# A hybrid RWKV-7 / S5 layer on one core: GpSimd's key products, PSUM tiles of one bank, the merge's loads and the rank of the chain

## The chip, the core and the metric

The kernel runs on one NeuronCore of a Trainium2 chip. The core has five engines that work at the same time, each through its own queue in order: TensorE (PE in the profile; its weight loads are listed as PEld), VectorE (DVE), ScalarE (ACT), GpSimd (POOL) and SyncE (SP), which here only starts DMA transfers. GpSimd starts some transfers too. Operands lie in SBUF, matmul results in PSUM, which has eight banks of 512 float32 columns on 128 partitions. GpSimd doesn't read PSUM in this kernel.

The metric is the device time of one execution in microseconds (us). Lower is better.

## What is computed

One decoder layer in float32 for 1024 positions of width 1024. The part that the change touches is the RWKV-7 branch: 8 heads of 64, with a state matrix per head that is decayed and corrected at every position, merged with an S5 branch under two gates.

```python
h = rms_norm(x, norm_mix_pre)
proj = h @ w_in                     # r, k, v, low-rank downs | S5 input | two gates
...
a = sigmoid(a0 + ad @ a2)
kk = k * k_k; kk = kk / norm(kk)    # per head
k = k * (1.0 + (a - 1.0) * k_a)
y = wkv7_scan(r, decay, k, v, -kk, kk * a)
y = groupnorm(y) * lnx_w + lnx_b
bonus = sum(r * k * r_k, axis=-1) * v
o_rwkv = ((y + bonus) * g) @ w_branch_rwkv
...
mixed = (g_rwkv * o_rwkv + g_s5 * o_s5) @ w_out
x = x + rms_norm(mixed, norm_mix_post)
f = conv_ffn(rms_norm(x, norm_ffn_pre), w_up, conv_w, conv_b, w_down)
x = x + rms_norm(f, norm_ffn_post)
```

## The kernel before

**Number format.** Large products are done as three matmuls: each float32 operand is split into a high part and a remainder (`split`, lines 226 and 227: a cast on ScalarE, a subtraction on VectorE), and high x high, high x low and low x high are added up (`mm3_steps`, lines 172 to 174). Weights are loaded as `wf` by SP, cast on ScalarE (line 156) and subtracted on VectorE (line 157). One step of `mm3_steps`, three matmuls of 128x128 by 512 columns, is called a projection step below.

**Stages.** Norm, S5 batches and the first projections; then the RWKV stage (`front_half`, second part), in which the remaining projections run as filling between the small matmuls of the RWKV branch; then the output projection, the norms and the feed-forward part.

**The RWKV stage.** It makes four passes `d`, i = 0 to 3: two groups of four heads (`g`), two halves of the sequence (`th`). For a pass,

- two *fronts* (`rwkv_front`, one for each pair of heads, u = 0 and 1) load k, tz (decay) and ta (the in-context rate) and later r and v, build the scaled keys and queries `bk` and `ar` (each [128, 8 chunks, 128], two halves of 64 columns), multiply them on TensorE into the masked matrices `gr` (line 702, evicted on line 705), and make the bonus term: a product of r, r_k and the new key, summed over each head by a matmul with a block matrix of ones (line 715). In the kernel before, the new key is made in `ta` by GpSimd (lines 690 and 691) and the product is VectorE's (line 713);
- `rwkv_inv` inverts the 32x32 diagonal blocks on VectorE (lines 760 and 762), taking them out and back through DRAM with GpSimd's DMAs (lines 710, 753, 765, 772). It is issued after the second front's end;
- `rwkv_nat` transposes keys and values, and `rwkv_level` puts the 64x64 inverse together: transposes on VectorE (line 784), two rounds of small matmuls (lines 791 and 799) with ScalarE copies between them (793 and 801);
- `rwkv_chain` goes through the eight chunks of 64 positions in order. A chunk has three bursts of small matmuls: line 832 (state S times `ar`), line 841 and the next chunk's lines 814 to 818 (`chain_v`), lines 849 and 851. Between the bursts ScalarE copies p1 (834), VectorE copies U (843) and updates S (853), ScalarE scales S (837) and copies the result yn (856). Each burst needs the eviction before it;
- `rwkv_out` normalises, adds the bonus, multiplies by g and stores the branch's result to `YR` in DRAM.

**What sets the order.** TensorE's queue has exactly the order in which the program issues its matmuls (`manual_schedule`). `drive` issues it: three lanes (the chain lane with nat, level, chain and out; two prep lanes with the fronts) and a list of fillings `self.fill` (projection steps). A lane yields a cost and a due time, and, where there is a third value, a factor. The planner has a clock `now` and a credit. A lane's step is issued if its due time is reached and the credit isn't negative; it takes 0.8 (`PACE`) x cost x factor from the credit. Otherwise one projection step is issued, which adds 0.68 to the clock and to the credit, up to 2.0 (`CREDIT`). A chain burst yields 0.6, 1.0, 0.6 with a due time of 0.8 (`T_CH`) after it. The inverse has a due time of 36.

The other engines' queues are put in order by a scheduler: among the instructions that are ready by its model, the one with the highest priority goes first. A priority is the place in the program, raised by `high_priority`: the prep lanes by `HP` (100000), the chain lane by `HP2` (200000), the fillings and `load_w` by `HPW` (400000). The inverse is issued under `HPW` too.

**The fillings of this stage.** What is left of the r, k, v projections, then 14 gate tiles one by one and two together (`gate_tiles(14, 15)`, 32 projection steps), and, put in by the chain lane after pass 1, `merge` (gates times branch results, with the S5 branch's GLU, 80 steps) and `outproj` (64 steps); after pass 3's `rwkv_nat`, `merge_s5`. `merge` begins by loading four tiles of `YR` (line 1083, by SP) into buffers with the tag `ld`, of which there are ten, and splitting them.

**PSUM in this stage.** Two banks for projections (`gm`), two for `rp`, and the chain's `cz`: two tiles of two banks. A chunk's tile z is read as [2, 4, 2, 64]: index k = 0 (p1, S and U sums, first bank), k = 1 (results, second bank).

Of the kernel before, what the change touches and what calls it, by code (L numbers as in the profile page):

```python
# [71 lines left out]
class Kern:  # L72
# [40 lines left out]
    def cz(self):  # L113

        return self.psx.tile([128, 1024], F32, tag="cz", name=self.nm("cz"), bufs=2)
# [506 lines left out]
    def rwkv_setup(self):  # L622
        nc = self.nc
        self.S = [self.rk.tile([128, 2, 64], F32, name=f"S{g}") for g in range(2)]
        for g in range(2):
            nc.gpsimd.memset(self.S[g], 0.0)

# [14 lines left out]
    def rwkv_front(self, d, u):  # L642
# [18 lines left out]
        k, tz, ta = (ld(x) for x in (self.RKV[4 + p], self.TZ[p], self.TA[p]))  # L661
# [28 lines left out]
        G.tensor_scalar(ta, ta, self.ka_h[:, p:p + 1], self.ka_1[:, p:p + 1], ALU.mult, ALU.add)  # L690
        G.tensor_tensor(ta, ta, k, ALU.mult)
        G.tensor_tensor(bk1, c64(ta), c64(tz), ALU.mult)
# [20 lines left out]
        V.scalar_tensor_tensor(r, r, self.vec("r_k", p), ta, ALU.mult, ALU.mult)  # L713
        pb = self.rp()
        mm(pb, self.cst("ones_bd"), r, start=True, stop=True)
# [58 lines left out]
    def rwkv_level(self, d):  # L774
# [3 lines left out]
        gr = d["gr"]  # L778
        p = self.cz().rearrange("p (u k c t) -> p u k c t", u=2, k=2, t=32)
# [8 lines left out]
        for u in range(2):  # L788
            for c in range(8):
                for h in range(2):  # L790
                    mm(p[hi[h], u, 0, c], gr[lo[h], u, c, h, 32:64], xz[lo[h], u, c], start=c == 0, **kw)
            for h in range(2):
                A.copy(xz[hi[h], u], p[hi[h], u, 0])
            yield 0.6, 0.3, 2.5
        yield 0, T_LV
        for u in range(2):
            for c in range(8):
                for h in range(2):
                    mm(p[lo[h], u, 1, c], xz[hi[h], u, c], gr[hi[h], u, c, h, 32:64], start=c == 0, **kw)
            for h in range(2):  # L800
                A.copy(gr[lo[h], u, :, h, 32:64], p[lo[h], u, 1])
# [3 lines left out]
    def chain_v(self, d, c):  # L805
# [3 lines left out]
        z = d["z", c] = self.cz().rearrange("p (k n u i) -> p k n u i", k=2, n=4, i=64)  # L809
        kw = dict(stop=True, skip_group_check=True)  # L810
        for u in range(2):
            for h, own in enumerate(HALF):
                sl = HALF[1 - h]
                mm(z[own, 0, 0, u], gr[sl, u, c, h, 0:64], V[sl, c, u], start=u == 0, **kw)
                mm(z[sl, 1, 0, u], gr[sl, u, c, h, 64:128], V[sl, c, u], start=u == 0, **kw)
            for h, own in enumerate(HALF):
                sl = HALF[1 - h]
                mm(z[own, 0, 1, u], bkn[sl, u, c, h], V[sl, c, u], start=False, **kw)

    def rwkv_chain(self, d):  # L820
# [6 lines left out]
        for c in range(8):  # L827
            z = d.pop(("z", c))
            for u in range(2):
                for k in range(2):  # L830
                    for h, sl in enumerate(HALF):
                        mm(z[HALF[h ^ k], k, 0, u], ar[sl, u, c, 64 * k:64 * k + 64], S[sl, u], **kw)
            p1 = self.small.tile([128, 2, 64], F32, tag="p1", name=self.nm("p1"), bufs=1)
            A.copy(p1, z[:, 0, 0])
# [3 lines left out]
            yield 0.6, T_CH  # L838
            for u in range(2):
                for h, sl in enumerate(HALF):  # L840
                    mm(z[sl, 0, 2, u], gr[sl, u, c, h, 0:64], p1[sl, u], **kw)
            U = self.small.tile([128, 2, 64], F32, tag="U", name=self.nm("U"), bufs=1)
            V.tensor_copy(U, z[:, 0, 2])
# [1022 lines left out]
```

## Time and profile before

| | before |
|---|---|
| median of 3 runs | 1634.47 us (1628.8 to 1636.94) |
| the profiled execution | 1641.13 us |
| its span, first to last instruction | 1638.7 us |
| its mean granted TensorE clock | 0.953 |
| TensorE busy | 1520.3 us, 93% |
| VectorE busy | 1124.7 us, 69% |
| ScalarE busy | 696.7 us, 43% |
| GpSimd busy | 146.1 us, 9% |

The profiled execution is one of its own, 2.4 us longer than its span and 6.7 us longer than the median of the runs; sums over its rows are made against its own time. RWKV's first front begins at about 270 us, and pass 3's chain ends at 786 us.

How to read the rows: `L713` is line 713 of the kernel before. A name on the left of `<-` is the tile that is written, names on the right are read. In a row of the timeline the first number is the start in us from the span's beginning, the second the length, `xN` the number of instructions in it, and a bracket tells how long the engine was idle before it and what ended that idle time. In a row of the waits stand the total, the number of times and the longest. Tiles with the tag `ld` all appear as `ld`, and a front's scratch space in `gr` appears as `gr`. PEclk is the TensorE clock that the throttle granted, as a share of full speed.

### The profile page before, as it was taken

The numbers are of one execution on the slowest core, as the hardware profiler recorded it, in microseconds if no ns is written. First come the engines' busy times: TensorE is split into PE (matmuls) and PEld (weight loads), VectorE is DVE, ScalarE is ACT, GpSimd is POOL, SyncE is SP. The second block draws the span as 40 slices with busy tenths as digits, with TensorE's granted clock in tenths as the row PEclk, the third lists the DMA queues.
The fourth block names the chain that finished last, engine by engine and source line by source line (L and its number), as shares of the span: only waits on it lengthen the run. The fifth ranks groups of instructions, "written<-read, shape, count | busy, mean of one in ns | idle before, by whom it ended". The sixth has DMA issues, their size and how long they took to land. (4 is left out here: it accounts for less than half of the span.)

```text
span 1638.7 us, 26115 instructions
## 1 busy us (share of the span) xinstructions
PE 1520.3 (93%) x10028; PEld 1218.0 (74%) x10028; DVE 1124.7 (69%) x2043; ACT 696.7 (43%) x1109; POOL 146.1 (9%) x218
## 2 busy tenths in 40 slices
PE   5899899898998988889999899999999999999995
PEld 4688787676666766567778688888888888788784
DVE  6798764555364545655659668977777777778767
ACT  4345543123342332464443444544445444443451
POOL 2100001403123123010000000000000000000000
PEclk9799999999998989989989899999999999999997
DMA  5254344342351352564466354322222223962622
GB/s 175 69 147 137 92 127 151 93 139 78 98 174 44 104 158 62 153 155 136 160 201 211 137 166 142 130 90 78 90 78 84 93 81 126 314 234 89 229 93 103
DMA packets 133421, 213.85 MB, mean 130 GB/s; under 512 B 38656, under 2 KB 44800, under 8 KB 133296
## 3 DMA queue, kind: packets, MB, share of 16 engines
q1 hardware_dynamic: 124208, 188.32, 35.1%
q0 software_dynamic: 7936, 21.77, 4.4%
q10 hardware_dynamic: 1152, 2.10, 0.3%
q8 instruction: 78, 1.28, 0.3%
q14 instruction: 47, 0.39, 0.1%
HBM read 156.56 MB, written 53.48 MB: 128 GB/s over the span
## 5 line engine op out<-in xcount | busy, mean ns | idle before, releaser
L172 PE MATMUL gm<-hh,wh 128*128 128x512 f32 x688 | 302.2, 439 | 13.4 <-ACT hh L226 9.5
L173 PE MATMUL gm<-hl,wh 128*128 128x512 f32 x688 | 282.8, 411 | 7.6 <-DVE hl L227 5.0
L174 PE MATMUL gm<-hh,wl 128*128 128x512 f32 x688 | 280.2, 407 | 0.0
L156 ACT CAST wh<-wf 128x512 fp32r<-128x512 f32 x179 | 110.8, 619 | 225.3 <-PE gm L173 135.4
L157 DVE TENSOR_TENSOR wl<-wf,wh 128x512 fp32r<-128x512 f32 x179 | 123.0, 688 | 101.4 <-ACT wh L156 99.9
L172 PEld LDWEIGHTS gm<-hh,wh 128*128 128x128 f32 x688 | 135.9, 198 | 51.7 <-ACT hh L226 12.1
L173 PEld LDWEIGHTS gm<-hl,wh 128*128 128x128 f32 x688 | 136.7, 199 | 36.4 <-DVE hl L227 8.3
L174 PEld LDWEIGHTS gm<-hh,wl 128*128 128x128 f32 x688 | 136.5, 198 | 30.4
L1491 PE MATMUL d<-xl,wh 128*128 128x512 f32 x308 | 120.8, 392 | 2.8 <-DVE xl L227 2.8
L1490 PE MATMUL d<-xh,wh 128*128 128x512 f32 x308 | 120.7, 392 | 2.1 <-ACT xh L226 2.1
L1492 PE MATMUL d<-xh,wl 128*128 128x512 f32 x308 | 120.6, 392 | 0.0
L1316 PE MATMUL rp<-t,h 128*128 128x512 f32 x216 | 84.4, 391 | 1.6 <-ACT p L1330 1.6
L1318 PE MATMUL rp<-t,l 128*128 128x512 f32 x216 | 84.2, 390 | 0.5 <-DVE l L227 0.5
L1317 PE MATMUL rp<-t,h 128*128 128x512 f32 x216 | 84.1, 389 | 0.0
L1491 PEld LDWEIGHTS d<-xl,wh 128*128 128x128 f32 x308 | 58.2, 189 | 16.2 <-DVE xl L227 4.1
L1490 PEld LDWEIGHTS d<-xh,wh 128*128 128x128 f32 x308 | 58.2, 189 | 14.7 <-ACT xh L226 2.4
L1492 PEld LDWEIGHTS d<-xh,wl 128*128 128x128 f32 x308 | 58.1, 189 | 11.9
L226 ACT CAST h<-r 128x1024 fp32r<-128x1024 f32 x34 | 35.8, 1054 | 61.1 <-PE rp L1317 29.6
L227 DVE TENSOR_TENSOR l<-r,h 128x1024 fp32r<-128x1024 f32 x34 | 41.6, 1225 | 29.3 <-ACT h L226 27.7
L837 ACT ACTIVATE spt<-S,pt 128x64 f32<-128x64 f32 x64 | 19.8, 342 | 78.2 <-DVE S L853 77.8
L1337 DVE SCALAR_TENSOR_TENSOR y<-zv,vecs,y 128x1023 f32<-128x1023 f32 (+1 forms) x36 | 46.1, 1281 | 8.6 <-ACT y L1335 8.6
L1316 PEld LDWEIGHTS rp<-t,h 128*128 128x128 f32 x216 | 40.5, 188 | 11.1 <-ACT p L1330 2.5
(436 smaller groups left out, 3383.7 us busy)
## 6 DMA issues: line engine op xcount, KB each, us to landing
r<-in_w_up_dram SPq DMA_DIRECT2D x36, 512.0 KB, 3.2
wf<-in_w_in_dram SPq DMA_DIRECT2D x68, 256.0 KB, 2.9
st<-in_w_down_dram SPq DMA_DIRECT2D x55, 256.0 KB, 4.2
st<-ACT SPq DMA_DIRECT2D x44, 256.0 KB, 4.6
wf<-in_w_up_dram SPq DMA_DIRECT2D x36, 256.0 KB, 2.8
ACT<-y POOLq DMA_DIRECT2D x18, 512.0 KB, 2.9
GT<-ev SPq DMA_DIRECT2D x32, 256.0 KB, 2.1
wf<-in_w_br_dram SPq DMA_DIRECT2D x32, 256.0 KB, 2.8
```

Of the source, the lines that this page charges most:

```text
L156: nc.scalar.copy(h[:, :n], f[:, :n])
L157: nc.vector.tensor_tensor(l[:, :n], f[:, :n], h[:, :n].bitcast(F32), ALU.subtract)
L172: mm(ps, a, xh[k], start=k == 0, stop=False)
L173: mm(ps, a, xl[k], start=False, stop=False)
L174: mm(ps, b, xh[k], start=False, stop=k == n - 1)
L1316: mm(ps, wh[:, c], xh, start=first and k == 0, stop=False, skip_group_check=True)
L1317: mm(ps, wh[:, c], xl, start=False, stop=False, skip_group_check=True)
L1318: mm(ps, wl[:, c], xh, start=False, stop=k == 3, skip_group_check=True)
L1337: V.scalar_tensor_tensor(y[:, lag:], z[:, 0:1024 - lag], self.vec(nme, i), y[:, lag:], ALU.mult, ALU.add)
L1490: mm(ps, wh[:, c], xh[:, x], start=start, stop=False, skip_group_check=True)
L1491: mm(ps, wh[:, c], xl[:, x], start=False, stop=False, skip_group_check=True)
L1492: mm(ps, wl[:, c], xh[:, x], start=False, stop=stop, skip_group_check=True)
```

## The change

Five edits.

1. **GpSimd's key products.** The new key k x (1 + (a-1) k_a) is built by GpSimd in `bk1`, the place where the scaled key will stand, instead of in `ta`, and it is issued right behind the loads of k and ta (whose order is changed: ta before tz). At the key stage GpSimd multiplies r by it and then scales it by tz in place. VectorE's product with r_k is gone: r_k is multiplied once into four block matrices `rkb`, which take the place of the matrix of ones in the bonus matmul.
2. **PSUM tiles of one bank.** `cz` gives two tiles of one bank each instead of one of two. All users index them as `z[0]`, `z[1]` (chain) or `p[0]`, `p[1]` (level).
3. **Wide work between the bursts.** Two of the three yields of a chunk have the factor 2.0.
4. **The merge's loads.** `merge_loads`, a filling without cost, stands ahead of the last two gate tiles. It issues the four loads of `YR` if two passes have been put out (`self.outs`); `merge` issues them itself if that hasn't been done.
5. **The chain lane's rank.** It is raised by `HPC` = 450000 instead of 200000.

```diff
     def cz(self):
 
-        return self.psx.tile([128, 1024], F32, tag="cz", name=self.nm("cz"), bufs=2)
+        return [self.psx.tile([128, 512], F32, tag=f"cz{k}", name=self.nm("cz"), bufs=2) for k in range(2)]
...
+        self.rkb = self.rk.tile([128, 4, 128], F32, name="rkb")
+        for p in range(4):
+            nc.vector.tensor_scalar(self.rkb[:, p], self.cst("ones_bd"), self.vec("r_k", p), None, ALU.mult)
...
-        k, tz, ta = (ld(x) for x in (self.RKV[4 + p], self.TZ[p], self.TA[p]))
+        k, ta, tz = (ld(x) for x in (self.RKV[4 + p], self.TA[p], self.TZ[p]))
+        G.tensor_scalar(bk1, c64(ta), self.ka_h[:, p:p + 1], self.ka_1[:, p:p + 1], ALU.mult, ALU.add)
+        G.tensor_tensor(bk1, bk1, c64(k), ALU.mult)
...
         V.scalar_tensor_tensor(bk0, c64(kk), 0.5, c64(tz), ALU.mult, ALU.mult)
-        G.tensor_scalar(ta, ta, self.ka_h[:, p:p + 1], self.ka_1[:, p:p + 1], ALU.mult, ALU.add)
-        G.tensor_tensor(ta, ta, k, ALU.mult)
-        G.tensor_tensor(bk1, c64(ta), c64(tz), ALU.mult)
+        G.tensor_tensor(c64(r), c64(r), bk1, ALU.mult)
+        G.tensor_tensor(bk1, bk1, c64(tz), ALU.mult)
...
-        V.scalar_tensor_tensor(r, r, self.vec("r_k", p), ta, ALU.mult, ALU.mult)
         pb = self.rp()
-        mm(pb, self.cst("ones_bd"), r, start=True, stop=True)
+        mm(pb, self.rkb[:, p], r, start=True, stop=True)
...
-        p = self.cz().rearrange("p (u k c t) -> p u k c t", u=2, k=2, t=32)
+        p = [x.rearrange("p (k c t) -> p k c t", k=2, t=32) for x in self.cz()]
...
-        z = d["z", c] = self.cz().rearrange("p (k n u i) -> p k n u i", k=2, n=4, i=64)
+        z = d["z", c] = [x.rearrange("p (n u i) -> p n u i", n=4, i=64) for x in self.cz()]
...
-            yield 0.6, T_CH
+            yield 0.6, T_CH, 2.0
...
-            yield 0.6, T_CH
+            yield 0.6, T_CH, 2.0
...
+    def merge_load(self):
+
+        if self.outs >= 2 and not self.yr:
+            for k in range(4):
+                self.yr.append(self.tg("ld", NLD))
+                self.nc.sync.dma_start(self.yr[k], self.YR[k][:, 0:512])
+
+    def merge_loads(self):
+        self.merge_load()
+        yield 0
...
         br = []
+        self.merge_load()
         for k in range(4):
-            y = self.tg("ld", NLD)
-            nc.sync.dma_start(y, self.YR[k][:, 0:512])
             br.append(self.pair(0, k))
-            self.split(*br[k], y)
+            self.split(*br[k], self.yr[k])
...
-                    self.gate_tiles(14, 15)]
+                    self.merge_loads(), self.gate_tiles(14, 15)]
+                self.outs, self.yr = 0, []
...
-            self.drive([(HP2, self.chain_lane(mg)), (HP, self.prep_lane(0)), (HP, self.prep_lane(1))])
+            self.drive([(HPC, self.chain_lane(mg)), (HP, self.prep_lane(0)), (HP, self.prep_lane(1))])
...
             yield from self.rwkv_out(d)
+            self.outs += 1
```

The remaining lines of the diff only write the new index of the PSUM tiles.

32 lines of the change are left out of this document (16 added, 16 removed).

## Prediction

> **What bounds the kernel now.** I read the page first: engine shares, then the slices.
>
> ```profile
> span 1638.7 us, 26115 instructions
> PE 1520.3 (93%) x10028; PEld 1218.0 (74%) x10028; DVE 1124.7 (69%) x2043; ACT 696.7 (43%) x1109; POOL 146.1 (9%) x218
> PE   5899899898998988889999899999999999999995
> PEclk9799999999998989989989899999999999999997
> ```
>
> TensorE is busy 93% of the span and runs its queue in an order written by hand, so a microsecond in which it waits is a microsecond of the kernel, unless a later wait swallows it. Slices are 41 us; the dips that the diff can touch lie between 280 us and 740 us, where the RWKV passes run inside the projections. So next the waits of TensorE, 280 to 800 us (total, times, longest):
>
> ```profile
> PE cz L832 <- DVE S L853: 12.4, 5, 4.3
> PE cz L791 <- DVE ld L784: 6.0, 5, 2.1
> PE gm L172 <- ACT hh L226: 5.8, 1, 5.8
> PE cz L849 <- DVE U L843: 5.4, 4, 1.8
> PE rp L702 <- DVE gr L705: 5.0, 1, 5.0
> PE cz L791 <- ACT ld L793: 5.0, 1, 5.0
> PE cz L799 <- ACT gr L801: 3.1, 3, 1.6
> PE rp L742 <- ACT bkn L736: 3.1, 1, 3.1
> ```
>
> Three of these (L832, L849, L702) happen at one place, the key stage of a front. Queues of VectorE, then GpSimd, at the second front (start, length, ..., idle before):
>
> ```profile
> 398.42 1.86 DVE L713 SCALAR_TENSOR_TENSOR ld<-ld,vecs,ld 128x512 f32<-128x512 f32 x1 [1.96 <-POOL ld L691]
> 400.21 0.28 DVE L843 COPY U<-cz 128x128 f32<-128x128 f32 x1
> 403.84 1.85 DVE L713 SCALAR_TENSOR_TENSOR ld<-ld,vecs,ld 128x512 f32<-128x512 f32 x1 [2.02 <-POOL ld L691]
> 406.21 0.46 DVE L853 SCALAR_TENSOR_TENSOR S<-cz,pt,spt 128x64 f32<-128x64 f32 x2
> ...
> 395.37 1.65 POOL L690 TENSOR_SCALAR ld<-ld,ka_h,ka 128x512 f32<-128x512 f32 x1 [12.91 <-DVE gr L688]
> 397.11 1.28 POOL L691 TENSOR_TENSOR ld<-ld,ld 128x512 f32<-128x512 f32 x1
> 398.47 1.27 POOL L692 TENSOR_TENSOR bk<-ld,ld 128x512 f32<-128x512 f32 x1
> ```
>
> GpSimd may not overwrite `ta` (L690) before VectorE has read it (L688); VectorE's bonus product L713 then waits for GpSimd's L691 and itself lasts 1.86 us. Behind it in VectorE's queue stand the chain's U copy and S update, and TensorE waits for these (its own rows):
>
> ```profile
> 307.11 2.58 PE L702 MATMUL rp<-ar,bk 64*64 64x128 f32 x32 [4.98 <-DVE gr L705]
> 400.55 0.27 PE L849 MATMUL cz<-U,bkn 64*64 64x64 f32 x2 [1.70 <-DVE U L843]
> 406.54 0.54 PE L832 MATMUL cz<-S,ar 64*64 64x64 f32 x16 [3.95 <-DVE S L853]
> 686.67 0.79 PE L172 MATMUL gm<-hh,wh 128*128 128x512 f32 x1 [5.77 <-ACT hh L226]
> 723.61 1.07 PE L791 MATMUL cz<-ld,gr 32*32 32x32 f32 x32 [4.95 <-ACT ld L793]
> ```
>
> The same happens at every front. Busy time by stage (length, PE, PEld, DVE, ACT, POOL, PEclk, ...): the key stages of fronts 0 to 3, an undisturbed stretch of chain, and from the last chain burst of pass 2 and of pass 1 to the first of the next pass:
>
> ```profile
> 301.03:312.34 11.31, 6.33 (x71) 4.54 (x70) 6.33 (x9) 0.00 (x0) 2.73 (x3) 0.70 0.20 71
> 396.39:414.50 18.11, 12.46 (x202) 9.51 (x201) 10.04 (x17) 4.19 (x12) 7.06 (x7) 0.91 0.12 40
> 508.94:527.51 18.57, 12.44 (x202) 9.61 (x201) 10.02 (x17) 3.58 (x11) 7.65 (x7) 0.91 0.12 44
> 621.70:639.87 18.17, 12.49 (x202) 9.33 (x201) 9.52 (x16) 3.25 (x11) 7.57 (x7) 0.91 0.13 45
> 430.06:448.70 18.64, 18.64 (x223) 13.12 (x222) 7.18 (x26) 6.64 (x19) 1.64 (x4) 1.00 0.47 132
> 674.45:736.32 61.87, 47.02 (x481) 35.07 (x475) 44.09 (x106) 37.84 (x64) 7.18 (x12) 0.83 0.67 173
> 562.09:614.38 52.29, 47.34 (x513) 36.87 (x507) 28.88 (x99) 20.57 (x39) 11.55 (x20) 0.87 0.45 140
> ```
>
> **The change part by part.**
>
> *GpSimd's key work.* L690 and L691 now write `bk1` instead of `ta` and need only `k` and `ta`, so they run as soon as these two loads land, and their wait for L688 is gone. L713 is gone (8 x 1.86 = 14.9 us of VectorE); GpSimd multiplies r by bk1 instead, and r_k sits in the weights `rkb` of the bonus matmul, which keeps its size. In TensorE's waits nothing is left at this stage that GpSimd holds: the products it still has there (r x bk1, bk1 x tz, 1.27 us each by L692) need the exponential and r, which are there a dozen microseconds earlier, before the 12.91 us that GpSimd now idles. The gain is the idle time of the four windows, 11.31-6.33 = 4.98, 18.11-12.46 = 5.65, 6.13 and 5.68, together 22.4 us, and the clock after it: busy work at 0.70 or 0.91 which the undisturbed window does at 1.00, 0.30 x 6.33 + 3 x 0.09 x 12.46 = 5.3 us. Sum **27.7 us**. What stands in that cover's place: GpSimd does one more product per front, and its first two come before the `tz` step (L673) for which VectorE's scan waits. Two pairs of 1.65 + 1.28 put the scan back by up to 5.9 us; the exponential behind it is needed by L687 and by the keys; GpSimd's 12.91 us of idle time between L687 and L690 show how long before the keys it is ready, so I cost it at nothing; without that cover it would be 3 x 5.9 = 18 us (the first front has no chain beside it). The four set-up multiplies for `rkb` are VectorE work of a quarter of L713's size each, once, where VectorE idles: nothing.
>
> One price speaks against moving a product to GpSimd. In the quoted rows L713 begins 0.05 us before GpSimd's L692 and lasts 1.86 us, 0.59 us beside L692's 1.27. If each of the eight additional products held a VectorE instruction so, it would be 8 x 1.27 = 10.2 us; if none did, 0. I take 0, because they run where VectorE and the chain have least to do, and keep 10.2 for the range. The Trainium skill's page "SBUF — State Buffer", section "SBUF: two separate sides", says that a GpSimd instruction and a VectorE instruction with two SBUF inputs lock one shared port pair, the loser fully blocked; the row agrees, and by that rule alone the sum would be 22.5 instead of 32.7 us.
>
> *Wide work between bursts.* The third yield value 2.0 makes two of the three chain steps cost 0.96 of credit instead of 0.48 (0.8 x 0.6 x factor); a projection step gives 0.68, up to a balance of 2.0. Going through the planner's yields by hand: with the chain alone, two projection steps separate the bursts before and after, since the chain's due time of 0.8 asks for two anyway. With a front beside it the balance is negative more often: six more steps per such pass, 18 over passes 0 to 2. These steps are not added but taken from the projections' tail, where 63 steps of output projection remain after the last chain and 45 will. TensorE's work is the same, the bursts as many: 0 us. A loss would come if the fill ran dry; it doesn't.
>
> *Merge loads and the pass-2 to pass-3 stretch.* The four YR loads now stand 32 projection steps before the merge, and the merge starts 18 steps sooner against the chain, nine steps before pass 2's last burst instead of nine after. The 5.77 us at 686.67 goes. But the time does not all stay gone: the next thing due is pass 3's level, whose transposes wait for the inverse's result by DMA, and that clock runs from the front, not from the merge. Window 674.45 to 736.32 is 61.87 us; pass 1's, with the same 41 projection steps, 52.29, and that one still holds two bursts for the next front. These rows set the two ends:
>
> ```profile
> L667 PE MATMUL rp<-csts,gr 128*128 128x2 f32 x64 | 10.0, 280 | 0.0
> 719.64 0.89 DVE L784 STREAM_TRANSPOSE ld<-gr 32x256 f32<-32x256 f32 x2
> DVE ld L784 <- DMA gr<-xd: 24.3, 8, 10.5
> 717.55 1.09 ACT L1052 CAST e<-et 128x512 fp32r<-128x512 f32 x1
> 721.19 0.36 ACT L793 COPY ld<-cz 32x256 f32<-32x256 f32 x1
> ```
>
> A front's burst of L667 takes 10.0 / 8 = 1.25 us (eight bursts), so if pass 3 becomes like pass 1, 61.87 - 52.29 + 2.5 = 12.1 us are won. If the inverse lands as late as now, the last transposes still end at 720.5, and the matmuls that began at 723.61 can only begin 3 us sooner. Between 3 and 12.1 I take **7**: the merge's VectorE work and its loads now come earlier than the inverse's last third, but stay beside it. 2 us go off for new waits of the merge's first glu tile, whose inputs are now split on a ScalarE that also serves the chain (before, these waits were under 2 us).
>
> *Priority HPC.* The chain lane now outranks weight casts and projection evictions. It is what lets L793 start after the cast at 717.55 rather than at 721.19, and is within the 7. At L742 (3.1 us) the copy L736 stood behind an inverse's start copy on ScalarE; it may or may not overtake it: 0, up to 3.1 plus as much again in clock as in window one, 1.9. What is queued behind a chain operation that waits, a cast or an eviction, has half a projection tile of time (four steps, about 3 us) or more: 0.
>
> *One-bank PSUM tiles.* The same eight banks and the same instructions; each half is released by itself, but its next user comes a whole chunk later: 0.
>
> **Sum.** 27.7 + 7 - 2 = 32.7 us. The profiled execution took 1641.13 us, 2.4 more than its span; 1641.1 - 32.7 = 1608.4. That execution is 6.7 us slower than the median of the runs, 1634.47, so I forecast **1602 us**.
>
> **Rivals.**
>
> 1. *The levels swallow it.* Each pass's inverse may simply be late, and what the key stage wins is lost at L791. For: VectorE waits 24.3 us for `gr<-xd`, and TensorE already 6.0 us at L791. Against: the key stage ends before the front's last matmul, from which the inverse starts, so both ends move. If it holds for fronts 1 to 3, the gain left is front 0's 4.98 + 1.9 and some of the 7: 10 us, 1624.
>
> 2. *Everything comes.* 27.7 + 12.1 + 5.0 at L742: 45 us, 1589. For: all these waits are TensorE's own. Against: the inverse's delay in pass 3.
>
> 3. *GpSimd's queue turns on the level (slower).* The early products need loads; the inverse's own result goes out through GpSimd's queue, in order. If the two lanes' pairs are queued ahead of the result DMAs L772, these wait until the loads are in.
>
> ```profile
> 477.19 2.89 POOL L772 DMA_DIRECT2D gr<-xd  x5 [2.28 <-DMA xd<-x]
> 487.45 0.61 POOL L673 TENSOR_SCALAR ld<-ld 128x512 f32<-128x512 f32 x1 [5.66 <-DMA ld<-TZ]
> 589.52 4.62 POOL L772 DMA_DIRECT2D gr<-xd  x8 [2.82 <-DMA xd<-x]
> 598.48 0.61 POOL L673 TENSOR_SCALAR ld<-ld 128x512 f32<-128x512 f32 x1 [4.34 <-DMA ld<-TZ]
> ```
>
>  In pass 1 the loads are in at 487.45 where L772 went at 477.19: 10.3 us and 2 x 2.9 of products, 16 us later; pass 2 15 us; pass 0 taken alike, 16. All three levels, less what is won: 47 - 33 = 14 us slower, 1649. It decides itself by whether the pairs stand before or behind L772. Against: L673, with inputs loaded at the same moment, stands behind it everywhere now.
>
> 4. *The change doesn't do what it says.* VectorE's queue blocks the chain on something else, the scan behind a later L673 or a gr product, at the same price as L713 did: 18 us of the 27.7 come back, and the merge's gain goes to the level: 1625 to 1640, say 1632.
>
> **How the numbers follow.** Forecast 0.62 (1592 to 1615), levels swallow 0.13, everything 0.12, GpSimd's queue 0.07, no effect 0.06. A measurement of this kernel can tell about 0.5% from no change, 8 us: faster means below 1626.3, slower above 1642.6. Faster: 0.62 + 0.12 + 0.10 of the third case = 0.84; same: the other 0.03, the 0.06; slower 0.07. The range 1588 to 1624 leaves out rivals 3 and 4 and the edges of 1 and 2. Its upper end holds the forecast with the 10.2 us of held VectorE and a level that gives only 3 (1616), and rival 1; its lower end rival 2.
>
> **What would show it.** No L713 on VectorE, and at the four key stages L849, L832 and L702 without idle time before them, granted clock 1.00: that is worth 28 us. GpSimd's first two key products right after the loads, ahead of L673 and behind L772. The wait at the merge's first matmul gone, and a wait at pass 3's L791 on L784 in its place, smaller than 9 us. Chain bursts with two projection steps between them as before, more where a front runs beside. Wrong would be: new idle time before L791 at passes 1 and 2 of more than 3 us each, or VectorE waiting for GpSimd at L674 while U or S stand behind it.

## The result, and the profile after

| | before | after |
|---|---|---|
| median of 4 runs | 1635.47 us (1628.8 to 1636.94) | 1618.58 us (1613.18 to 1621.26) |
| the profiled execution | 1641.13 us | 1618.77 us |
| its span | 1638.7 us | 1616.8 us |
| granted clock | 0.953 | 0.962 |

The changed kernel takes 0.990 of the time before (95% interval 0.9863 to 0.9938): 16.9 us, or 1.0%, where 32.7 were forecast. The profiled executions are 22 us apart, because that of before lies 5.7 us above its median. Single executions of one kernel differ by up to 1%, and the granted clock with them (of the four of after, 1611.2 us of span went with 0.966, the other three, 1616.6 to 1619.0, with 0.958 to 0.962). A stretch of one trace is therefore taken as good to some 3 us only, and what an edit is worth is read from the ratios.

The page of after, in the lines shown of before:

```profile
span 1616.8 us, 26128 instructions
PE 1507.2 (93%) x10028; PEld 1206.2 (75%) x10028; DVE 1127.3 (70%) x2039; ACT 697.3 (43%) x1109; POOL 154.7 (10%) x226
PE   5899899898999989879988999999999999999995
PEclk9799999999999999979989999999999999999997
```

Of the slices that the diff can touch, the thirteenth (485 to 525 us) and the sixteenth (606 to 646) rose from 8 to 9, where key stages lie beside a chain; the eighteenth (687 to 727), on the way into pass 3, fell from 8 to 7. TensorE's waits, 280 to 800 us (total, times, longest):

```profile
PE cz L794 <- DVE ld L787: 17.1, 12, 7.6
PE rp L689 <- ACT gr L687: 8.4, 2, 4.7
PE rp L885 <- DVE yn L879: 4.3, 1, 4.3
...
PE rp L706 <- DVE gr L709: 0.9, 1, 0.9
```

The lines have moved by 3 to 5 (S is L835, keys L706, the level L794). The waits for S and U, 12.4 and 5.4 us before, are down to 0.4, that of the keys from 5.0 to 0.9, the merge's 5.8 is gone. In their place stand the level's transposes (17.1 instead of 6.0) and a new one: L689, the transposes of the fronts' norms, which waits for ScalarE's copy L687, and this for VectorE's inverse square root.

Busy time by stretch (length, PE, PEld, DVE, ACT, POOL, PEclk, ...), first before, then after: from the first to the eighth S burst of pass 0; from there to pass 1's first; pass 2, first to eighth; and on to pass 3's first:

```profile
388.69:444.73 56.04, 50.39 (x707) 35.97 (x706) 25.07 (x59) 16.01 (x46) 15.91 (x20) 0.97 0.27 77
444.73:499.69 54.96, 51.33 (x545) 39.31 (x544) 33.23 (x114) 21.38 (x42) 12.18 (x20) 0.88 0.43 140
613.99:670.08 56.09, 50.41 (x706) 35.79 (x705) 25.06 (x59) 15.90 (x46) 16.25 (x20) 0.97 0.27 76
670.08:736.32 66.24, 51.39 (x528) 38.13 (x527) 47.56 (x119) 38.98 (x67) 7.18 (x12) 0.85 0.63 164
```

```profile
386.02:441.25 55.23, 53.73 (x725) 38.04 (x724) 24.94 (x69) 17.16 (x48) 9.09 (x15) 1.00 0.31 90
441.25:492.52 51.27, 47.94 (x544) 37.08 (x544) 32.45 (x100) 21.46 (x43) 20.42 (x28) 0.93 0.48 150
595.92:657.35 61.43, 56.41 (x724) 39.60 (x724) 36.50 (x81) 29.15 (x65) 14.65 (x20) 0.94 0.44 125
657.35:723.06 65.71, 49.99 (x528) 37.85 (x527) 46.48 (x121) 30.77 (x56) 7.20 (x12) 0.82 0.52 142
```

Pass 0 holds 18 more matmuls (six projection steps) in less time, at full clock. Pass 2, with the same 18, has grown by 5.3 us, and the way into pass 3 is as long as before although the merge's wait is gone from it.

Where pass 2 loses time, the trace of after shows at the last front. VectorE, then GpSimd (start, length, ..., idle before), then who waits:

```profile
594.27 2.20 DVE L679 TENSOR_TENSOR_SCAN ld<-csts,ld 128x512 f32<-128x512 f32 x1 [2.79 <-POOL ld L678]
596.39 0.13 DVE L675 TENSOR_SCALAR sv<-rp 128x8 f32<-128x8 f32 x1
596.56 1.02 DVE L136 TENSOR_SCALAR rsy<-sv 128x8 int32<-128x8 int32 x1
...
597.82 1.12 DVE L139 TENSOR_TENSOR rsh<-rsy 128x8 f32<-128x8 f32 x1
598.98 1.11 DVE L140 SCALAR_TENSOR_TENSOR rsh<-rsh,sv 128x8 f32<-128x8 f32 x1
...
600.32 1.12 DVE L139 TENSOR_TENSOR rsh<-rsy 128x8 f32<-128x8 f32 x1
...
601.57 1.24 DVE L137 TENSOR_SCALAR rsy<-rsy 128x8 int32<-128x8 int32 x1
...
595.47 2.09 POOL L695 TENSOR_TENSOR ld<-ld,bk 128x512 f32<-128x512 f32 x1
597.63 1.29 POOL L696 TENSOR_TENSOR bk<-bk,ld 128x512 f32<-128x512 f32 x1
598.88 1.18 POOL L692 TENSOR_TENSOR ar<-ld,gr 128x512 f32<-128x512 f32 x1
...
600.16 1.26 POOL L695 TENSOR_TENSOR ld<-ld,bk 128x512 f32<-128x512 f32 x1
601.51 1.27 POOL L696 TENSOR_TENSOR bk<-bk,ld 128x512 f32<-128x512 f32 x1
...
603.52 0.62 ACT L687 COPY gr<-rsy 128x512 f32<-128x512 f32 x1 [4.85 <-DVE rsy L141]
604.19 1.11 PE L689 MATMUL rp<-csts,gr 128*128 128x128 f32 x4 [3.72 <-ACT gr L687]
```

Add start and length: the product L695 ends at 597.56, L136 at 597.58; L696 at 598.92, L139 at 598.94; L692 at 600.06, L140 at 600.09; and so on for all five. An instruction on 128x8 numbers, 0.17 us by itself, lasts until GpSimd's product beside it has ended. The root is a chain of eleven such instructions, one after the other, and the roots of the two head pairs stand mixed in VectorE's queue. Four instructions of the first root and one of the second, which stands between them, wait out a product: 5.61 us instead of 0.85. L675, which reads PSUM, takes 0.13 us. The Trainium skill's page "SBUF — State Buffer", section "SBUF: two separate sides", says it as a rule: of a GpSimd instruction and a VectorE instruction with two SBUF inputs or in a two-port mode, the one that starts first holds the shared port pair for its whole length and the other blocks. These rows agree, in that the instruction that started second is the one that waits; L136 and L137 have one input, and the rows don't tell whether they run in such a mode. It is the price that the prediction set between 0 and 10.2 us and took as 0.

### The profile page after: what moved, and what is told of

It reads as the page before. It is cut to its first block, busy times and chain, and to the rows that moved or that the text cites. A ratio compares the mean times of both kernels' runs of the same rounds, so it can differ in the third digit from the quotient of the medians.

```text
span 1616.8 us, 26128 instructions
## 1 busy us (share of the span) xinstructions
PE 1507.2 (93%) x10028; PEld 1206.2 (75%) x10028; DVE 1127.3 (70%) x2039; ACT 697.3 (43%) x1109; POOL 154.7 (10%) x226
## 4 chain that ended last, share of the span: by engine, by line
PE 68%; DVE 15%; DMA 8%; issue 4%; ACT 3%; POOL 2%; SPq 1%; DVEq 0%; ACTq 0%; POOLq 0%
PE gm L172 9%; PE gm L173 8%; PE gm L174 7%; PE rp L1329 4%; PE rp L1331 4%; PE rp L1330 4%; DMA st<-in_w_down_dram 2%; PE d L1504 2%; PE mm L1329 2%; PE mm L1330 2%; PE mm L1331 2%; PE d L1505 2%; PE d L1503 2%; PE ch L172 2%; PE ch L173 2%
## 5 line engine op out<-in xcount | busy, mean ns | idle before, releaser
L173 PE MATMUL gm<-hl,wh 128*128 128x512 f32 x688 | 279.3, 406 | 5.3 <-DVE hl L227 4.4
L174 PE MATMUL gm<-hh,wl 128*128 128x512 f32 x688 | 276.7, 402 | 0.0
L1504 PEld LDWEIGHTS d<-xl,wh 128*128 128x128 f32 x308 | 57.8, 188 | 17.1 <-DVE xl L227 5.2
L1331 PEld LDWEIGHTS rp<-t,l 128*128 128x128 f32 x216 | 40.8, 189 | 9.5 <-DVE l L227 1.0
```

What stands on the lines that cost most here:

```text
L173: mm(ps, a, xl[k], start=False, stop=False)
L174: mm(ps, b, xh[k], start=False, stop=k == n - 1)
L1331: mm(ps, wl[:, c], xh, start=False, stop=k == 3, skip_group_check=True)
L1504: mm(ps, wh[:, c], xl[:, x], start=False, stop=False, skip_group_check=True)
```

## The experiments

Stretches are read from the starts of rows in TensorE's timeline: *front 0* from its first norm matmul to its last key burst; *in pass* from the first to the eighth S burst of passes 0, 1, 2; *between* from the eighth to the first of the next pass; *into 3* the same from pass 2 to pass 3; *tail* from pass 3's eighth burst to the end. *Key work* is edit 1, *spacing* edit 3. Kernels marked s hold 18 more matmuls of six projection steps in a pass, about 5 us (pass 0 of run 14 takes 48.7, of run 12 53.7), and have 54 fewer in the tail; run 12 has them in passes 0 and 1 only, and 36 fewer in the tail.

| kernel | ratio to before (95%) | front 0 | in pass | between | into 3 | tail |
|---|---|---|---|---|---|---|
| before | 1 | 30.4 | 56.0 58.0 56.1 | 55.0 56.3 | 66.2 | 857.2 |
| after (s) | 0.9900 (0.9863 to 0.9938) | 31.6 | 55.2 54.2 61.4 | 51.3 49.2 | 65.7 | 849.3 |
| key work alone | 0.9955 (0.9938 to 0.9972) | 32.2 | 50.1 49.9 50.2 | 56.2 55.6 | 68.6 | 859.9 |
| after without key work (s) | 0.9876 (0.9846 to 0.9906) | 30.3 | 55.4 55.0 56.3 | 49.6 51.1 | 64.4 | 851.1 |
| after without spacing | 0.9882 (0.9845 to 0.9919) | 32.0 | 50.2 49.7 49.0 | 56.0 55.5 | 59.8 | 860.8 |
| after with neither | 0.9937 (0.9918 to 0.9957) | 30.2 | 56.1 57.9 55.8 | 48.3 52.9 | 64.1 | 860.2 |
| two passes' spacing, no products on GpSimd (s) | 0.9783 (0.9757 to 0.9810) | 26.3 | 53.7 55.7 49.8 | 53.8 53.1 | 62.2 | 852.2 |
| no spacing, no products on GpSimd | 0.9815 (0.9790 to 0.9840) | 28.4 | 48.7 49.8 49.2 | 55.1 53.0 | 62.9 | 861.0 |

**1. The key work alone** (the kernel before with edit 1)

```diff
+        G.tensor_scalar(bk1, c64(ta), self.ka_h[:, p:p + 1], self.ka_1[:, p:p + 1], ALU.mult, ALU.add)
+        G.tensor_tensor(bk1, bk1, c64(k), ALU.mult)
...
-        V.scalar_tensor_tensor(r, r, self.vec("r_k", p), ta, ALU.mult, ALU.mult)
...
+        mm(pb, self.rkb[:, p], r, start=True, stop=True)
```

> The kernel before with GpSimd's key work and the rkb weights alone; two-bank tiles, merge loads, chain priority and step costs as before. Theory A (the key work is what brings the 17 us, less what the first and last front give back): the two middle fronts lose their four waits for U and S, about 7 us each, the first and last front win 0 +- 2 us: 14 us off, 1618 to 1624, and TensorE waits 3 to 5 us for ScalarE's copy of the inverse norms (the L682 of before) at the first front. Rival B (the gain comes from the other edits, above all from the six more projection steps beside each front): under 6 us off, 1629 or more.

Measured: 1629.66 us beside 1636.78, 7.1 off: half of theory A's 14, and just over the 6 that rival B allowed. Passes 0 and 2 of this kernel by stretch, and TensorE's wait at its first front:

```profile
394.99:445.08 50.09, 50.09 (x706) 35.58 (x705) 20.78 (x53) 15.53 (x44) 7.92 (x14) 0.97 0.31 86
606.78:657.02 50.24, 50.00 (x707) 35.58 (x706) 23.86 (x65) 15.78 (x45) 9.97 (x16) 0.97 0.31 85
...
297.42 1.97 PE L689 MATMUL rp<-csts,gr 128*128 128x128 f32 x8 [5.46 <-ACT gr L687]
```

In the passes theory A is right and more: 56.04 + 58.03 + 56.09 became 50.09 + 49.86 + 50.24, 20.0 us won, and hardly any idle time. Around them 12 go again, for its span is 8.0 below before's: front 0 is 1.9 us longer, the way from there to pass 0 3.8, into 3 2.4, the tail 2.7.

**2. The changed kernel without the key work**

```diff
-        k, ta, tz = (ld(x) for x in (self.RKV[4 + p], self.TA[p], self.TZ[p]))
+        k, tz, ta = (ld(x) for x in (self.RKV[4 + p], self.TZ[p], self.TA[p]))
...
+        V.scalar_tensor_tensor(r, r, self.vec("r_k", p), ta, ALU.mult, ALU.mult)
```

> The changed kernel with GpSimd's key work as before (L713 back on VectorE); one-bank tiles, merge loads, chain priority and step costs as changed. Theory A: 2 to 6 us faster than before, 1629 to 1633; the waits for U and S at the key stages return at 5 us for each front, and at the last pass the wait of the level's matmuls for the transposes stays (7 us or more) because it hangs on the inverse, not on the key work. Rival B: 11 us faster or more, under 1624, with the waits at the key stages under 2 us although L713 stands there, since the wider spacing covers them.

Measured: 1616.64 us beside 1636.78, 20.1 off: rival B. L713 is back, and in pass 0 TensorE idles 1.31 us all the same:

```profile
387.65:443.01 55.36, 54.05 (x724) 38.27 (x723) 25.99 (x60) 17.02 (x48) 16.02 (x20) 1.00 0.30 82
```

So the wait at the key stage has two remedies in this change, and the one priced at 0 suffices.

**3. The copy of pt on ScalarE** (the changed kernel)

```diff
-        G.tensor_copy(d["pt"][:, :, u], pe[:, :, 64])
+        A.copy(d["pt"][:, :, u], pe[:, :, 64])
```

> The changed kernel with the small copy of pt (L683) on ScalarE behind its exponential, not on GpSimd. Theory A (at the first front the copy of the second half stands behind three moved products on GpSimd, the first chunk's spt waits for it at the head of ScalarE's queue, and the casts, evictions and the norm copy behind it are late): the 3.28 us of ScalarE before spt go, the wait of TensorE for L687 at the first front falls from 4.68 to under 2 us, that at the last front (3.72) stays within 1 us, because its rsqrt instructions are held by the products all the same; 4 to 6 us faster than the changed kernel, 1612 to 1615. Rival C (both stalls come from the tz step and the scan, late behind the first two products of each half): both stay, 1617 to 1620.

Measured: 1621.18 us, 0.9899 (0.9882 to 0.9916), nothing gained, and theory A falls. Both stalls stay (4.33 and 3.62 us), as rival C had it; the time is 1.2 us above its range. After's ScalarE row, then three of this run's:

```profile
286.82 0.35 ACT L840 ACTIVATE spt<-S,pt 128x64 f32<-128x64 f32 x1 [3.28 <-POOL pt L683]
```

```profile
284.44 2.20 DVE L679 TENSOR_TENSOR_SCAN ld<-csts,ld 128x512 f32<-128x512 f32 x1 [2.50 <-POOL ld L678]
287.22 0.33 ACT L840 ACTIVATE spt<-S,pt 128x64 f32<-128x64 f32 x1
297.12 1.97 PE L689 MATMUL rp<-csts,gr 128*128 128x128 f32 x8 [4.33 <-ACT gr L687]
```

ScalarE's 3.28 us are gone and TensorE's wait is not: the scan lasts 2.20 instead of 1.23 us, the root's first two steps 1.14 and 1.33 for a pair, beside GpSimd's products.

**4. The two later products on VectorE** (the changed kernel)

```diff
-        G.tensor_tensor(c64(r), c64(r), bk1, ALU.mult)
-        G.tensor_tensor(bk1, bk1, c64(tz), ALU.mult)
+        V.tensor_tensor(c64(r), c64(r), bk1, ALU.mult)
+        V.tensor_tensor(bk1, bk1, c64(tz), ALU.mult)
```

> The changed kernel with the two later products (r x bk1 and bk1 x tz) on VectorE at their place in the code, the first two on GpSimd as changed. Theory A (GpSimd's products hold VectorE: the 128x8 rsqrt instructions of the last front last 1.02 to 1.24 us instead of 0.17): they last 0.17 to 0.3 us, the stall before L689 at the last front (3.72) falls under 1 us, and with GpSimd's queue short the one at the first front (4.68) too; VectorE has 16 x 0.69 = 11 us more work and the time is 1608 to 1613. Rival D (VectorE's place at the key stage is what counts, as with L713): its 1.4 us more per half come back before L706 and the chain's U and S, 2 to 4 us per front, 1620 to 1630.

Measured: 1611.46 us beside 1636.78, 0.9841 (0.9807 to 0.9874). The root's instructions are back at 0.17 us, both waits at L689 are gone, front 0 takes 28.4 us and pass 2 takes 56.6 instead of 61.4: theory A. Two of the root's instructions at the last front, held in after:

```profile
592.65 0.16 DVE L136 TENSOR_SCALAR rsy<-sv 128x8 int32<-128x8 int32 x1
...
595.29 0.15 DVE L139 TENSOR_TENSOR rsh<-rsy 128x8 f32<-128x8 f32 x1
```

VectorE has 16 products of 0.69 us more, 11 us, and is busy no longer than in after (1127.0 us against 1127.3). The gain over the changed kernel is 0.6%, and the two intervals still touch.

**5. The spacing alone** (the kernel before)

```diff
-            yield 0.6, T_CH
+            yield 0.6, T_CH, 2.0
```

(both yields of that form in `rwkv_chain`)

> The kernel before with the two step costs of the chain (the third yield value 2.0) alone; L713 and GpSimd's key work as before. Theory F (six more projection steps beside each front give VectorE the time that L713 takes, so that TensorE no longer reaches U and S too early): from the first to the eighth S burst of passes 0, 1 and 2, where before was idle for 5.6, 6.1 and 5.7 us, TensorE is idle for under 2.5 us each; 12 to 18 us faster, 1619 to 1625. Rival G (what the prediction said: the steps only move, 0 us): the idle time at the key stages is within 1.5 us of before's, 1633 to 1640.

Measured: 1620.22 us beside 1638.05, 0.9903 (0.9871 to 0.9934): theory F. Idle time in passes 0 and 1 is 1.3 and 0.8 us. Its profiled execution is its slowest (1629.09); pass 2 idles 4.5 us there, theory F's one miss.

**6. The changed kernel without the spacing**

```diff
-            yield 0.6, T_CH, 2.0
+            yield 0.6, T_CH
```

> The changed kernel with the chain's step costs as before; key work, one-bank tiles, merge loads and priority as changed. Theory F (spacing and key work take away the same waits, so that either does without the other): passes 0 and 1 have no idle time from the first to the eighth S burst (as with the key work alone, 50.1 and 49.9 us), the changed kernel's stall before L689 at the first front stays at 4 to 5.5 us, and the time is 1620 to 1628: between the key work alone (1629.7) and the changed kernel. Rival H (spacing brings time of its own, by the clock or at the levels, and the other three edits nothing): the same time as the key work alone, 1628 to 1632, with 55 to 57 us between the eighth burst of a pass and the first of the next.

Measured: 1618.78 us, the time of the changed kernel; 0.9882 (0.9845 to 0.9919), below F's range by 1 us. Passes 0 and 1 idle 1.5 and 1.0 us. Not expected was the way into pass 3:

```profile
648.28:708.09 59.81, 49.83 (x529) 36.96 (x528) 43.32 (x113) 35.29 (x59) 7.18 (x12) 0.89 0.63 164
```

59.81 us, 6.4 below before, with 10.0 us of idle time instead of 14.9 and a granted clock of 0.89.

**7. The priority alone, 8. the merge loads alone, 10. the one-bank tiles alone** (each the kernel before with that edit)

```diff
-            self.drive([(HP2, self.chain_lane(mg)), (HP, self.prep_lane(0)), (HP, self.prep_lane(1))])
+            self.drive([(HPC, self.chain_lane(mg)), (HP, self.prep_lane(0)), (HP, self.prep_lane(1))])
...
-                    self.gate_tiles(14, 15)]
+                    self.merge_loads(), self.gate_tiles(14, 15)]
...
-        return self.psx.tile([128, 1024], F32, tag="cz", name=self.nm("cz"), bufs=2)
+        return [self.psx.tile([128, 512], F32, tag=f"cz{k}", name=self.nm("cz"), bufs=2) for k in range(2)]
```

> The kernel before with the chain's priority 450000 (ahead of casts and evictions) alone. From the eighth burst of a pass to the first of the next before took 55.0 and 56.3 us, the changed kernel without its key work 49.6 and 51.1, with the same projection steps and a clock of 0.97 and 0.93 instead of 0.88. Theory I (the priority does that: evictions and casts no longer stand ahead of a level's copies): these two stretches fall to 49 to 52 us, 6 to 11 us faster, 1626 to 1631. Rival J (it is the spacing that leaves the front earlier done and the level later due): they stay at 54 to 57 us, 1633 to 1640.

> The kernel before with the early loads of the merge alone. Theory K (the merge's wait is swallowed: the level of pass 3 waits for the inverse's result in any case): the 5.8 us wait of the merge's first matmul is gone, the stretch from the last burst of pass 2 to the first of pass 3 is 65 to 68 us as before (66.2), with the idle time at the level's matmuls instead; 1633 to 1639. Rival L (the prediction's): that stretch falls by 5 to 8 us, to 58 to 61, and the time to 1626 to 1632.

> The kernel before with the one-bank tiles alone. Theory O (no one waits for a half bank pair): the stretches between the bursts are within 1.5 us of before's, and the time within 4 us of it: 1633 to 1641. Rival P (a chunk's second half, released by itself, lets the next chunk's V products start earlier): the wait of S and U at the key stages falls by 1 us or more each, 1626 to 1632.

Measured: 0.9981 (0.9953 to 1.001), 0.9973 (0.9949 to 0.9998) and 0.9936 (0.9912 to 0.9959). The priority's two stretches stay at 56.7 and 55.6 us (rival J); the way into pass 3 falls to 59.4 us with it, to 62.0 with the loads (between K and L), and to 63.1 with the tiles. The tiles were costed at 0 and are worth some 10 us by the ratio: P's time, but not P's mark, for the idle time in the passes fell by 0.2 to 0.8 us, and the profiled execution (1634.23) is that kernel's slowest. What they release earlier stays open. The three together, run 13, are worth no more than the tiles alone.

**9. The spacing in passes 0 and 1 only** (the changed kernel)

```diff
+        w = 2.0 if d["th"] == 0 else 1.0
...
-            yield 0.6, T_CH, 2.0
+            yield 0.6, T_CH, w
```

> The changed kernel with the wider step costs in passes 0 and 1 only, as before in pass 2. Theory M (the wider spacing of pass 2 starts the merge earlier against pass 3's inverse, whose VectorE steps it then sits between): from the last burst of pass 2 to the first of pass 3, 65.7 us in the changed kernel and 59.8 without any wider spacing, 59 to 62 us, with the wait of the level's matmuls for the transposes under 5 us instead of 11; pass 2 itself 4.8 us shorter for its six steps less, the tail 3 to 5 longer; 4 to 7 us faster than the changed kernel, 1611 to 1615. Rival N (that stretch hangs on the inverse's own clock; 59.8 came from passes 0 and 1): 64 to 67 us, and 1617 to 1621.

Measured: 1615.24 us beside 1639.61, 0.9848 (0.9820 to 0.9876). Into pass 3 62.9 us, out of M's range and out of N's, but the idle time there is 14.6 us, as in the changed kernel, and the level's wait still 7.52 in one piece: M falls, and it isn't pass 2's spacing alone. The gain over the changed kernel, 0.5%, is less than the two intervals can part.

**11 and 12. Key products off GpSimd, with the spacing of run 9**: in run 11 the two later ones on VectorE, in run 12 the first two as well:

```diff
-        G.tensor_scalar(bk1, c64(ta), self.ka_h[:, p:p + 1], self.ka_1[:, p:p + 1], ALU.mult, ALU.add)
-        G.tensor_tensor(bk1, bk1, c64(k), ALU.mult)
...
+        A.activation(bk1, c64(ta), AF.Identity, bias=self.ka_1[:, p:p + 1], scale=self.ka_h[:, p:p + 1])
+        V.tensor_tensor(bk1, bk1, c64(k), ALU.mult)
```

> The wider step costs in passes 0 and 1 only, together with the two later key products on VectorE. If M and the held VectorE (theory A of the run with the products on VectorE) are both right and at different places, their gains add: 5 us for the one, 7 for the other, 1604 to 1608, with no idle time before L689. If they hang on one thing: 1610 to 1614, no better than the better one.

> As the one before, with the first two key steps off GpSimd too: the scale and offset of ta (L665) on ScalarE, its product with k (L666) on VectorE. If the two early products put the tz step and with it the scan and the norms of the first front back (2.1 us of idle time before L689 were left there with the later two alone on VectorE), that idle time goes, the scans last 1.23 us, and the time is 1602 to 1606. If VectorE's additional 8 x 0.69 us hold the fronts instead, the idle time moves to L706 or to U and S, and the time is 1607 or more.

Measured: run 11 took 1612.67 us, 0.9828 (0.9804 to 0.9853), no better than run 4 within the intervals, and TensorE's wait at L689, expected to be gone, is 5.2 us. Run 12 took 0.9783 (0.9757 to 0.9810), 1604.79 us: the fastest here, 10 us below run 9, from which it differs only in the engine of four key steps. VectorE's groups, 270 to 720 us (busy, mean ns of one, idle before and whose), of before, of after and of run 12:

```profile
L674 DVE TENSOR_TENSOR_SCAN ld<-csts,ld 128x512 f32<-128x512 f32 x8 | 9.8, 1224 | 15.3 <-POOL ld L673 15.2
L136 DVE TENSOR_SCALAR rsy<-sv 128x8 int32<-128x8 int32 x8 | 1.3, 170 | 0.1
```

```profile
L679 DVE TENSOR_TENSOR_SCAN ld<-csts,ld 128x512 f32<-128x512 f32 x8 | 13.3, 1662 | 19.9 <-POOL ld L678 19.8
L136 DVE TENSOR_SCALAR rsy<-sv 128x8 int32<-128x8 int32 x8 | 4.8, 616 | 0.1
```

```profile
L679 DVE TENSOR_TENSOR_SCAN ld<-csts,ld 128x512 f32<-128x512 f32 x8 | 9.7, 1217 | 1.5 <-POOL ld L678 1.5
L136 DVE TENSOR_SCALAR rsy<-sv 128x8 int32<-128x8 int32 x8 | 2.2, 284 | 0.1
```

Front 0 falls to 26.3 us, 4.1 below before; a wait of 1.86 us at its L689 is left, and one of 1.08 at the last front.

**13. Neither key work nor spacing, 14. no spacing and no products on GpSimd** (13 joins the edits of runs 2 and 6, 14 those of 6, 4 and 12)

```diff
-            yield 0.6, T_CH, 2.0
+            yield 0.6, T_CH
...
-        G.tensor_tensor(c64(r), c64(r), bk1, ALU.mult)
-        G.tensor_tensor(bk1, bk1, c64(tz), ALU.mult)
+        V.tensor_tensor(c64(r), c64(r), bk1, ALU.mult)
+        V.tensor_tensor(bk1, bk1, c64(tz), ALU.mult)
```

> The changed kernel with neither the key work nor the wider step costs: one-bank tiles, merge loads and priority alone. With the three runs there are (both 0.9900 of before, key work alone added 0.9882, spacing alone added 0.9876) this is the fourth corner. Theory F (key work and spacing take away the same waits): the waits for U and S return, 5 to 6 us of idle time in each of the three stretches from a pass's first burst to its eighth, 59 to 62 us from the last burst of pass 2 to the first of pass 3, and 0.993 to 0.997 of before, so that each of the two alone is worth 8 to 14 us on top of it and the second nothing. Rival Q (neither is worth anything beside the three others): within 4 us of 0.988.

> As the run with no key products on GpSimd, and the chain's step costs as before in all passes. Theory F (with the key stage free of waits the wider spacing has nothing left to cover): the stretches from first to eighth burst 49 to 51 us without idle time, the one into pass 3 59 to 61, the first front 26 to 27 us as in the run before, the tail 10 us longer than with spacing; time within 5 us of that run, 0.975 to 0.982 of before. Rival R (the two passes' spacing is worth time at the levels, 56 to 50 us between the eighth burst of a pass and the first of the next): 0.983 to 0.988.

Measured: 0.9937 (0.9918 to 0.9957), theory F: idle time in the passes 5.7, 7.4 and 5.4 us again. Its way into pass 3 takes 64.1 us, 2 above what was expected. And run 14 took 0.9815 (0.9790 to 0.9840): inside theory F's range, though front 0 (28.4) and the way into pass 3 (62.9) are not; the intervals don't part it from run 12. In its trace, passes 0 and 1 with the stretches behind them take 206.6 us, in run 12's 216.3, and the tail is 8.8 longer: there the spacing only moves the steps.

The four corners, beside the other three edits: neither 0.9937, key work 0.9882, spacing 0.9876, both 0.9900. Each is worth 0.55% to 0.61%, some 9 us, and the second nothing. The interval of neither parts from that of the spacing, touches that of the key work and overlaps that of both, so these values are good to some 0.4% only.

## Why the prediction was wrong by half

**The key work, 27.7 us: the wait was read rightly, what it costs to remove it was not.** In run 1 the three passes won 20.0 us and the key bursts of the first front 6.2 (13.9 before from the first to the last, 7.7 now): 26.2 of 27.7. But run 1's span is only 8.0 us below before's: 18 of the 26 went again, 8.1 of them in the first front ahead of its key bursts (24.5 us from its first norm matmul to its first key burst, 16.4 before). The step that failed is the pair of prices beside it: the port lock, "I take 0", and the early products, "I cost it at nothing", argued from GpSimd's idle time. Idle time of GpSimd says nothing on what its work does to VectorE. Its products run just when VectorE makes the norms, in instructions too short to be seen in a sum of busy time. Of the 88 instructions of the four fronts' roots 12 last 0.6 to 1.3 us in after, as many in run 1 and in run 6, each ending 0.02 to 0.03 us after a product; in before none does, in runs 4 and 11 none, in 12 and 14 two. Taking the four steps off GpSimd, to ScalarE and VectorE, and nothing else, brings 0.67% (run 6 to run 14) and 0.65% (run 9 to run 12), each clear of the intervals: 11 us where 0 stood. The bounds of 10.2 and 18 were worked out and passed over. By the rule of the Trainium skill's page "SBUF — State Buffer" ("SBUF: two separate sides") the sum would have been 22.5, the nearer one. The rows that the prediction read there agree with the block, not with who wins: all eight L713 start 0.04 us before GpSimd's L692 and still end 0.55 us after it, at 1.85 to 1.88 us where L688 of the same size takes 0.68. So VectorE was held in before too.

The 11 us are what the four steps cost on GpSimd, not what the held instructions alone cost; that division isn't shown. The later two steps alone brought 0.6% from after to run 4 and 0.2% from run 9 to run 11, neither clear of the intervals. In run 11 no root instruction is held, and TensorE waits 3.47 us at the last front's L689 all the same: VectorE's own L695 and L696 now stand between the root's steps. At the first front of after one root instruction is held, for 0.9 us; ahead of it VectorE waits 3.84 us for a cast that had stood on ScalarE behind GpSimd's copy of pt, and when run 3 took that away, the wait at L689 stayed.

**The spacing, 0 us: wrong as a mechanism.** Alone it is worth 16 us (run 5). The credits were followed rightly, 18 steps into the passes and out of the tail, but a step beside a front is no neutral work: it gives VectorE the time that L713 takes, and TensorE comes to U and S when they are there. The sum thus held one wait with two remedies. On top of the key work the spacing brings nothing that the intervals show (0.9882 without it, 0.9900 with it).

**The merge and the way into pass 3, 7 less 2 us: 0.5 came.** The merge's 5.77 us are gone and the level's wait is there in their place: 7.65 + 0.51 + 0.98 + 2.32 = 11.5 us at pass 3's L794, more than the 9 that the prediction allowed, and 4.26 at L885:

```profile
706.19 0.31 PE L794 MATMUL cz<-ld,gr 32*32 32x32 f32 x2 [7.65 <-DVE ld L787]
707.01 1.05 PE L794 MATMUL cz<-ld,gr 32*32 32x32 f32 x30 [0.51 <-DVE ld L787]
...
710.62 0.31 PE L794 MATMUL cz<-ld,gr 32*32 32x32 f32 x2 [0.98 <-DVE ld L787]
...
713.25 1.06 PE L794 MATMUL cz<-ld,gr 32*32 32x32 f32 x30 [2.32 <-DVE ld L787]
```

Over the runs the idle time of this stretch (14.9 before) falls in two groups: 9 to 11 us in the six kernels that have an edit other than the key work and no spacing (runs 6, 7, 8, 10, 13, 14), 13 to 16 in all that have the spacing, in passes 0 and 1 alone too (runs 9, 11 and 12). So 4 to 6 us of idle time are there to be had, as the term said, and with the spacing they stay. In length, where the clock comes in, the groups overlap: 59.4 to 64.1 us without the spacing, 64.4 to 65.9 with it in three passes, 62.2 to 62.9 with it in two. "The merge starts 18 steps sooner" had been written down as a gain; sooner, it may meet pass 3's inverse, which no run tests by itself. The inverse's first and last product, 31 of them, in run 6 and then in after:

```profile
647.20 0.22 DVE L763 TENSOR_TENSOR tm<-x,mt 128x62 f32<-128x62 f32 x1
681.08 0.18 DVE L763 TENSOR_TENSOR tm<-x,mt 128x16 f32<-128x16 f32 x1
```

```profile
656.28 0.23 DVE L763 TENSOR_TENSOR tm<-x,mt 128x62 f32<-128x62 f32 x1
693.14 0.18 DVE L763 TENSOR_TENSOR tm<-x,mt 128x16 f32<-128x16 f32 x1
```

34.1 us without the spacing, 37.0 with it, and the transposes that wait for its result end 50.2 and 55.9 us after pass 2's last S burst. Over all runs the inverse takes 33.0 to 36.7 us without the spacing and 36.7 to 38.7 with it, so the other edits move it too (36.7 in run 7, 36.2 in run 10).

**The rivals.** The levels (first rival) take a part, by single traces: in run 6 TensorE takes 56.0 and 55.5 us from one pass to the next where the kernel with neither edit takes 48.3 and 52.9; the spacing wins that back in after (51.3, 49.2). GpSimd's queue (third) didn't turn: its first products stand behind the inverse's result DMAs at every front. The fourth was nearest in kind: VectorE is blocked by something else, by the products beside it instead of its own queue, and the 18 us that it let come back are, in size, what run 1 gave back.

**The sum again.** 32.7, less 11 for the steps on GpSimd, less 4.5 into pass 3: 17, and 16.9 were measured. That it fits so well is luck. Measured part by part, the key work is worth 7 us alone and 9 beside the three other edits, not 17, and these three are worth 10 together (run 13), where the sum has 5 less 4.5. The stretches between the passes won 10.8 us that no term held, and the tail gave back 7.9 where the 54 matmuls moved out of it took 15 in the passes. Why the tail gives less isn't known. The one-bank tiles, costed at 0, are worth some 10 us alone and little of that beside the others.

## What to carry to other kernels

Before work goes to GpSimd, look at what VectorE does in the same microseconds, short dependent instructions above all: here each could wait out a whole product, so VectorE's loss goes by their number and not by their length. If two edits of one change both touch a wait, price it once, and ask of every "neutral" step that is moved whose time it covers. The best kernel of this study keeps the freed key stage and takes the four key steps to VectorE and ScalarE (0.978 of before with the spacing in two passes, 0.982 without it, not told apart).

## What the runs showed that was not expected

An instruction of 0.17 us on 128x8 numbers lasted 1.02 to 1.24 us beside a product of GpSimd, and ended 0.02 to 0.03 us after it, five times in 7 us. The products suffer too: L695 took 2.09 instead of 1.26 us where VectorE's scan held it. Run 14 gives VectorE 24 products of 0.69 us more than run 6 has, 17 us, and VectorE is busy no longer (1126.0 us against 1126.4), for its instructions aren't held any more; the kernel is 0.67% shorter.
